# Last pair of up chunks of a streaming-encoder block as a seven-product block pair, with the first tiles of the down product placed on bytes of the pair's operands

## The chip, the cores and the metric

The kernel runs on one core of one Trainium2 chip. The metric is the device time of one execution in microseconds (us). The engines: TensorE (PE) multiplies matrices, VectorE (DVE), ScalarE (ACT) and GpSimd (POOL) do the elementwise work, SyncE (SP) issues most transfers. A time of the trace counts from the first instruction of the profiled execution.

## The reference

The kernel computes one layer of an encoder on 16 meta tokens and 1,024 positions, width 1,024: a mixer (attention with forget gates beside a diagonal state-space model), then a gated feed-forward block with a short causal convolution, then a norm. The change is in the feed-forward block:

```python
def _conv_ffn(xn, w_up, conv_w, conv_b, w_down):
    seq_len = xn.shape[1]
    hid = xn @ w_up
    hp = jnp.pad(hid, ((0, 0), (CONV_WIDTH - 1, 0), (0, 0)))
    conv = conv_b + sum(hp[:, j:j + seq_len] * conv_w[j] for j in range(CONV_WIDTH))
    val, gate = jnp.split(conv, 2, axis=-1)
    return (jax.nn.silu(gate) * val) @ w_down
```

`w_up` is 1024 x 5632, `w_down` 2816 x 1024, all in float32. The layer adds this to its input `h`, the norm is applied to the sum, and the meta tokens are dropped.

## The kernel before

A product of float32 precision is made of three matmuls: each operand is split into a high part (a cast to fp32r on ACT) and a low part (the operand less its high part, a subtraction called a cut here, `split_lo`, L137), and high x high, high x low and low x high are added up in PSUM.

**Up stage.** The 5,632 hidden channels are 22 chunks of values (`ov`) and 22 chunks of gates (`og`), 128 channels each; pair c is value chunk c with gate chunk c. Pairs 0, 1, 2 and 21 are *plain* (`plain_steps`, L1338 to L1366): for each of the two chunks and each of three stretches of 342 positions, 8 slices of the input width times 3 matmuls (L1357 to L1359); the convolution reads PSUM, one activation (L1361) and two products (L1363) for each stretch. Pairs 3 to 20 are *block pairs* (`block_pair`, L1490): the two chunks and the two halves of the positions form a 2 x 2 block product that is made with seven products instead of eight (`seven`, L214; matmuls L236 to L238, additions L242, copies L245 and L250). It reads blocks of the normed input `xhi`/`xlo` (`B11`, `B21`, `B22`; `B12` is not read as such) and four combined blocks `T` (t0 to t3, high and low, 65,792 bytes of each partition, pool `tforms`). The order of the seven is: A11 with B11, S2 with t1, A12 with B21, S3 with t2, S1 with t0, A22 with t3, S4 with B22, two pieces of 258 and 256 columns each. Weight forms are sums on POOL (L1451), casts (L1304) and cuts, in a ring of eight slots (`sw`). Results lie whole in `hg` and `hv`, and one activation and two products for each chunk (L1501, L1503) make the convolution. `glue` (L1311) then applies Silu to the gate, multiplies and stores the chunk to `a_d` in DRAM; for the pairs of `SUMMED` it also stores combined halves to `s_d`.

**Down stage.** The second matmul is again a block product with seven products p, over 11 pairs of rows j = 2c, 2c+1 in four groups: (8, 9), (7, 0, 1), (2, 3, 4), (5, 6, 10). "(g, p)" is product p of group g; the order within a group is 0, 4, 1, 2, 5, 3, 6. `forms(p, j)` loads a weight tile (`wr`, tag "w") and, for a `SUMMED` j, a combined activation tile (`ar`, tags a00 to a11), casts both on ACT (L1583) and cuts them, on POOL for p = 0, 4 and 5, on DVE for the others. The results go into a *slot* of four 128 x 512 tiles; slots are taken from the list `ops` and given back when the product has run. Slots are tiles `op0` to `op5` and quarters of the dead `xhi` and `xlo` (`featq`). `product` runs 4 row tiles x (row pairs of the group) x 3 matmuls of 512 columns (L1697 to L1699) and evicts: (0, 0) by copies on ACT into `u2` (L1702), (0, 1) and (0, 5) by ACT into `hs4` to `hs7` (L1705), all others by additions on DVE (L1707) into `hs`. `hs0` to `hs3` start with the residual, loaded from `h_d` (L1769). Products 4, 5 and 6 add onto PSUM banks of products 0, 1 and 3, so that these must be evicted before.

The order of instructions of an engine is set at build time by a list scheduler from the order of the program, buffers and data; `after(a, b)` adds an order between two instructions. Each engine, and each transfer queue, works in its order. Memory is a stack of pools from the left and from the right; a tile placed on bytes of an earlier one waits for that tile's last use. Before the change `tforms` is closed ahead of the plain pair 21, `down1` (`op0` to `op3`, weights, a tiles) takes its bytes from there on, and `dn` (`gfB`, `sq`, `eps`, `u2`, `hs`, `op4`, `op5`) lies from the end of `down1` over the bytes of the up stage's right side (`st_r`).

## Time and profile before

| | us |
|---|---|
| median of 3 runs | 1427.48 |
| the three runs | 1426.45, 1427.48, 1427.57 |
| the profiled execution, whole time | 1427.24 |
| its span, first to last instruction | 1425.5 |
| granted TensorE clock, mean | 0.998 |

The whole time of the profiled execution contains its span and 1.7 us around it. In a line of a timeline the first number is the start in us, the second the duration, then engine, line, operation, output<-input and shape; what stands in brackets is the idle time of the engine just before and what ended it. A line ending in "q" after the engine's name (SPq) is a transfer's issue. In a group of a line the three numbers behind the count are shortest, median and longest duration in ns.

### The profile page before, as it was taken

The numbers are of one execution on the slowest core, as the hardware profiler recorded it, in microseconds if no ns is written. First come the engines' busy times: TensorE is split into PE (matmuls) and PEld (weight loads), VectorE is DVE, ScalarE is ACT, GpSimd is POOL, SyncE is SP. The second block draws the span as 40 slices with busy tenths as digits, with TensorE's granted clock in tenths as the row PEclk, the third lists the DMA queues.
The fourth block names the chain that finished last, engine by engine and source line by source line (L and its number), as shares of the span: only waits on it lengthen the run. The fifth ranks groups of instructions, "written<-read, shape, count | busy, mean of one in ns | idle before, by whom it ended". The sixth has DMA issues, their size and how long they took to land.

```text
span 1425.5 us, 26319 instructions
## 1 busy us (share of the span) xinstructions
PE 1410.6 (99%) x9607; PEld 1336.1 (94%) x9607; DVE 1070.3 (75%) x2048; ACT 709.0 (50%) x1381; POOL 764.2 (54%) x872
## 2 busy tenths in 40 slices
PE   8999999999999999999999999999999999999997
PEld 8999999988999999999889999999999999888886
DVE  7999889843667675655479977788886776788867
ACT  7647575423555555534546444344444345644444
POOL 1542257642466556326771334545555545888795
PEclk9999999999999999999999999999999999999999
DMA  8685644530156531087953246666753327864443
GB/s 298 176 203 147 160 106 133 172 119 31 53 156 161 127 111 57 23 287 267 216 161 124 73 114 183 183 173 177 178 142 113 98 79 258 327 205 133 129 94 118
DMA packets 93318, 216.17 MB, mean 152 GB/s; under 512 B 14802, under 2 KB 22610, under 8 KB 92804
## 3 DMA queue, kind: packets, MB, share of 16 engines
q1 hardware_dynamic: 74340, 170.28, 36.3%
q0 software_dynamic: 17696, 41.29, 15.1%
q10 hardware_dynamic: 1152, 2.91, 0.7%
q8 instruction: 76, 1.25, 0.4%
q14 instruction: 54, 0.44, 0.1%
HBM read 170.88 MB, written 71.71 MB: 170 GB/s over the span
## 4 chain that ended last, share of the span: by engine, by line
PE 95%; DMA 2%; issue 1%; ACT 1%; DVE 0%; POOL 0%; POOLq 0%; DVEq 0%; SPq 0%
PE mm L174 5%; PE mm L176 5%; PE mm L175 5%; PE sp L236 4%; PE sp L237 4%; PE sp L238 4%; PE tp L236 3%; PE tp L237 3%; PE tp L238 3%; PE mm L238 3%; PE mm L236 3%; PE mm L237 3%; PE po L966 3%; PE tp L920 2%; PE mm L1699 2%; PE mm L1698 2%
## 5 line engine op out<-in xcount | busy, mean ns | idle before, releaser
L174 PE MATMUL mm<-xhi,whi 128*128 128x342 f32 (+2 forms) x480 | 156.1, 325 | 0.0
L175 PE MATMUL mm<-xlo,whi 128*128 128x342 f32 (+2 forms) x480 | 155.4, 324 | 0.0
L176 PE MATMUL mm<-xhi,wlo 128*128 128x342 f32 (+2 forms) x480 | 154.6, 322 | 0.5 <-DMA wlo<-in_w_g_dram 0.5
L1313 POOL TENSOR_TENSOR ov<-ov,og 128x1024 f32<-128x1024 f32 x21 | 50.8, 2421 | 119.7 <-ACT og L1312 117.4
L137 DVE TENSOR_TENSOR sw<-sf,sw 128x512 fp32r<-128x512 f32 x72 | 73.4, 1020 | 46.2 <-ACT sw L1304 45.1
L1304 ACT CAST sw<-sf 128x512 fp32r<-128x512 f32 x72 | 44.9, 624 | 108.9 <-POOL sf L1451 80.1
L176 PEld LDWEIGHTS mm<-xhi,wlo 128*128 128x128 f32 x480 | 90.4, 188 | 1.3 <-DMA wlo<-in_w_g_dram 0.8
L174 PEld LDWEIGHTS mm<-xhi,whi 128*128 128x128 f32 x480 | 90.4, 188 | 1.1 <-issue 0.6
L175 PEld LDWEIGHTS mm<-xlo,whi 128*128 128x128 f32 x480 | 90.4, 188 | 0.4
L1451 POOL TENSOR_TENSOR sf<-raw,sf 128x512 f32<-128x512 f32 x36 | 62.9, 1748 | 38.8 <-DVE sw L137 38.7
L1451 POOL TENSOR_TENSOR sf<-raw 128x512 f32<-128x512 f32 x36 | 49.1, 1363 | 60.0 <-ACT ov L1361 21.5
L238 PE MATMUL mm<-xhi,sw 128*128 128x258 f32 (+1 forms) x288 | 81.0, 281 | 0.0
L236 PE MATMUL mm<-xhi,sw 128*128 128x258 f32 (+1 forms) x288 | 80.8, 280 | 0.0
L237 PE MATMUL mm<-xlo,sw 128*128 128x258 f32 (+1 forms) x288 | 80.7, 280 | 0.0
L883 ACT ACTIVATE pt<-pt,mx 128x400 f32<-128x400 f32 (+5 forms) x72 | 53.1, 737 | 45.2 <-DVE mx L876 44.9
L1503 DVE SCALAR_TENSOR_TENSOR ov<-hv,cwt,ov 128x1024 f32<-128x1024 f32 x36 | 69.9, 1942 | 0.4 <-ACT ov L1501 0.4
L885 POOL TENSOR_SCALAR pt<-pt,mx 128x400 f32<-128x400 f32 (+5 forms) x72 | 51.8, 721 | 33.3 <-DVE mx L884 28.3
L1304 ACT CAST sw<-raw 128x512 fp32r<-128x512 f32 x70 | 43.0, 621 | 45.0 <-PE sp L238 23.1
L137 DVE TENSOR_TENSOR sw<-raw,sw 128x512 fp32r<-128x512 f32 x70 | 57.9, 831 | 4.3 <-ACT sw L1304 4.0
L137 DVE TENSOR_TENSOR tl<-tp,th 128x512 fp32r<-128x512 f32 (+1 forms) x80 | 50.7, 634 | 12.2 <-ACT th L923 11.6
L923 ACT CAST th<-tp 128x512 fp32r<-128x512 f32 (+1 forms) x80 | 43.4, 543 | 32.1 <-PE tp L920 22.7
L852 POOL CAST qz<-q 64x128 fp32r<-64x128 f32 (+1 forms) x72 | 20.2, 283 | 67.2 <-PE sp L871 65.7
(722 smaller groups left out, 5727.2 us busy)
## 6 DMA issues: line engine op xcount, KB each, us to landing
raw<-in_w_up_dram SPq DMA_DIRECT2D x44, 512.0 KB, 3.7
t_d<-in_w_dn_dram POOLq DMA_DIRECT2D x44, 256.0 KB, 6.9
wr<-t_d SPq DMA_DIRECT2D x44, 256.0 KB, 3.4
ar<-a_d SPq DMA_DIRECT2D x41, 256.0 KB, 5.3
a_d<-ov SPq DMA_DIRECT2D x18, 512.0 KB, 2.6
wr<-in_w_dn_dram SPq DMA_DIRECT2D x33, 256.0 KB, 3.8
t_d<-in_w_dn_dram SPq DMA_DIRECT2D x22, 256.0 KB, 4.3
t_d<-t_d SPq DMA_DIRECT2D x22, 256.0 KB, 4.7
```

The costliest lines, as they stand in the source:

```text
L137: return eng.tensor_tensor(out_, src, hi.bitcast(F), ALU.subtract)
L174: yield PE.matmul(ps, whi[:, i, :], ahi[:, i], start=(i == 0), stop=False)
L175: yield PE.matmul(ps, whi[:, i, :], alo[:, i], start=False, stop=False)
L176: yield PE.matmul(ps, wlo[:, i, :], ahi[:, i], start=False, stop=(i == k - 1))
L236: PE.matmul(ps, a[0][:, i], bh, start=(i == 0 and not joins), stop=False, skip_group_check=True)
L237: PE.matmul(ps, a[0][:, i], bl, start=False, stop=False, skip_group_check=True)
L238: PE.matmul(ps, a[1][:, i], bh, start=False, stop=(i == kh - 1), skip_group_check=True)
L883: ends[:] = rd, S.activation(pt[:n, :kc], pt[:n, :kc], AF.Exp, bias=low, scale=-1.0, accum_out=nm[:n, 0:1])
L885: sc_.append(GP.tensor_scalar(pt[:n, :kc], pt[:n, :kc], nm[:n, 1:2], 1.0, ALU.mult, ALU.mult))
L1304: S.copy(hi, src)
L1451: sums.append(GP.tensor_tensor(f_, a, b, op))
L1503: V.scalar_tensor_tensor(out=o, in0=h_[:, j:SEQ + j], scalar=cwc(j, m), in1=o, op0=ALU.mult, op1=ALU.add)
```

## The change

Pair 21 becomes a block pair. `block_pair` is cut in two: the products, and `conv_pair` with the convolution and the glue. `tforms` now stays open through pair 21, and its tiles are placed in the order t1, t2, t0, t3. A small pool `down0` (two weight tiles, two a00 tiles, `eps`) is placed below it, so that it shares no bytes with the up stage. `down1` is placed on the bytes of T in the order weights, a01, `op0`, `op1`, a10, a11, `hs0` to `hs3`, `u2`. The first slots are quarters of `xhi`/`xlo` that the block pairs read no more. At the border the order is: forms (0, 0), products of pair 21, forms (0, 4) and (0, 1), loads of `hs0` to `hs3`, product (0, 0), convolution and glue of pair 21, then the remaining products. Of pair 21's convolution the values come first; the gate's two products on DVE stand behind the cuts so far, the Silu behind the four copies of (0, 0), the first four additions of `hs` behind the gate's last product, the casts of (0, 3) and (0, 6) behind the evictions of (0, 1), the loads of group 0 one behind the other and ahead of the `hs` loads and of group 1, and the cuts of (1, 0) behind those of (0, 5). The last chunk's store goes to POOL's queue instead of ACT's.

```diff
     def glue(g_, v_, c):
-        S.activation(g_, g_, AF.Silu)
+        silu = S.activation(g_, g_, AF.Silu)
+        for cp_ in first_copy:
+            after(silu, cp_)
...
-        (S if c == NFF - 1 else SY).dma_start(rows, v_)
+        (GP if c == NFF - 1 else SY).dma_start(rows, v_)
...
     def conv_out(m, tag):
-        if m % NFF == NFF - 1:
-
-            return ha.tile([P, SEQ], F, tag="h", name=tag, bufs=3, padded_shape=[P, 2 * NH])
...
+    down0 = pool(ctx, "down0", side="left")
+    for tag in ("a00", "w"):
+        down0.tile([P, 512], F, tag=tag, name="hold", bufs=2)
+    eps = down0.tile([P, 1], F, name="eps")
+    V.memset(eps, EPS)
     st_t = ExitStack()
     tq = pool(st_t, "tforms", side="left")
-    T = [[tq.tile([P, KH, NH], R, name=f"t{i}{w}") for w in "hl"] for i in range(4)]
+    T = {i: [tq.tile([P, KH, NH], R, name=f"t{i}{w}") for w in "hl"] for i in (1, 2, 0, 3)}
+    T = [T[i] for i in range(4)]
...
-        res = []
-        for h_, m, tag in ((hg, NFF + c, "og"), (hv, c, "ov")):
-            o = conv_out(m, tag)
+        return hg, hv
+
+    def conv_pair(c, hg, hv, behind=()):
+        res = {}
+        halves = ((hg, NFF + c, "og"), (hv, c, "ov"))
+        for h_, m, tag in halves[::-1] if behind else halves:
+            res[tag] = o = conv_out(m, tag)
             S.activation(o, h_[:, :SEQ], AF.Identity, bias=cwc(3, m), scale=cwc(0, m))
             for j in (1, 2):
-                V.scalar_tensor_tensor(out=o, in0=h_[:, j:SEQ + j], scalar=cwc(j, m), in1=o,
-                                       op0=ALU.mult, op1=ALU.add)
-            res.append(o)
-        glue(*res, c)
+                st_ = V.scalar_tensor_tensor(out=o, in0=h_[:, j:SEQ + j], scalar=cwc(j, m), in1=o,
+                                             op0=ALU.mult, op1=ALU.add)
+                if tag == "og":
+                    for cut in behind:
+                        after(st_, cut)
+                    last_gate[:] = st_,
+        glue(res["og"], res["ov"], c)
...
     for c in range(3, NFF - 1):
-        block_pair(c)
-    st_t.close()
-    plain_pair(NFF - 1)
...
-    down1 = pool(ctx, "down1", side="left")
-    small = [down1.tile([P, 4, 512], R, name=f"op{q}") for q in range(4)]
-    ops = [[t_[:, w] for w in range(4)] for t_ in small]
-    ops += featq
-    dpool = {}
+        conv_pair(c, *block_pair(c))
+
+    def quarter(r, h_):
+        cols = slice((L - 512) * h_, (L - 512) * h_ + 512)
+        return [[t_[:, KH * r + 2 * q + w, cols] for w in range(2) for t_ in (xhi, xlo)] for q in range(2)]
+
+    ops = quarter(0, 1)
...
     def behind(ld, j):
-        if h_load and j in groups[1]:
+        if h_load and len(first_loads) == 12:
             after(ld, h_load[-1])
+        if j in groups[1]:
+            after(ld, first_loads[-1])
+        if j in groups[0]:
+            if first_loads:
+                after(ld, first_loads[-1])
+            first_loads.append(ld)
...
+            if j in groups[0] and p in (3, 6):
+                late_casts.append(hi)
+            elif j in groups[0] and p == 5:
+                fifth[:] = cut,
+            elif j in groups[1] and p == 0:
+                after(cut, fifth[0])
...
+                ev = S.activation(to, ps, AF.Copy, scale=-1.0 if p in MINUS else 1.0)
+                if p == 1:
+                    for hi in late_casts:
+                        after(hi, ev)
             else:
                 first_add.append(V.tensor_tensor(to, to, ps, ALU.subtract if p in MINUS else ALU.add))
+                if len(first_add) <= 4:
+                    after(first_add[-1], last_gate[0])
...
+    ready[0, 0] = [forms(0, j) for j in groups[0]]
+    last_pair = block_pair(NFF - 1)
+    st_t.close()
+    down1 = pool(ctx, "down1", side="left")
     dpool[0] = down1
-    for p in ORDER[:2]:
+    down1.tile([P, 512], F, tag="w", name="hold", bufs=6)
+    down1.tile([P, 512], F, tag="a01", name="hold", bufs=2)
+    small = op_tiles(down1, 0, 2)
+    for tag in ("a10", "a11"):
+        down1.tile([P, 512], F, tag=tag, name="hold", bufs=2)
+    hs = {c: down1.tile([P, D], F, name=f"hs{c}") for c in range(4)}
+    u2 = [down1.tile([P, 512], F, name=f"u2{c}") for c in range(4)]
+    ops += small + quarter(0, 0) + quarter(1, 0)
+    for p in (4, 1):
         ready[0, p] = [forms(p, j) for j in groups[0]]
+    for c in range(4):
+        h_load.append(SY.dma_start(hs[c], h_d[P * c:P * c + P]))
+        after(h_load[-1], first_loads[-1])
+    product(0, 0, ready[0, 0], True, False)
+    conv_pair(NFF - 1, *last_pair, behind=cuts)
     st_r.close()
     dn = pool(ctx, "down", side="left")
...
+    ops += op_tiles(dn, 2, 4) + quarter(1, 1) + op_tiles(dn, 4, 6)
+    hs.update((c, dn.tile([P, D], F, name=f"hs{c}")) for c in (4, 5))
+    cuts.clear()
+    ops += ready[0, 0]
+    for g, p in turns[1:]:
         prepare()
```

More of the change, by code (lines that the diff above doesn't have):

```diff
@@ L1512, in block_kernel, with weight_tile, raw_buffer, op_tiles @@
     for c in range(3, NFF - 1):
-        block_pair(c)
-    st_t.close()
-    plain_pair(NFF - 1)
-    down1 = pool(ctx, "down1", side="left")
-    small = [down1.tile([P, 4, 512], R, name=f"op{q}") for q in range(4)]
-    ops = [[t_[:, w] for w in range(4)] for t_ in small]
-    ops += featq
-    dpool = {}
+        conv_pair(c, *block_pair(c))
[3 more added lines that the diff above has]
+    ops = quarter(0, 1)
+    n_w = [0]
+    def weight_tile():
+        n_w[0] += 1
+        if n_w[0] % 8 in (1, 2):
+            return down0.tile([P, 512], F, tag="w", name="wr", bufs=2)
+        return down1.tile([P, 512], F, tag="w", name="wr", bufs=6)
+    def raw_buffer(j, tag):
+        pl = dpool[turn_of[j] % 4 // 2]
+        if pl is dpool[0] and tag == "a00":
+            pl = down0
+        return pl.tile([P, 512], F, tag=tag, name="ar", bufs=2)
+    def op_tiles(pl, q0, q1):
+        small = [pl.tile([P, 4, 512], R, name=f"op{q}") for q in range(q0, q1)]
+        return [[t_[:, w] for w in range(4)] for t_ in small]
+    dpool = {0: None}
     pairs = {}
@@ L1593, in forms @@
         return slot
[L1595 removed]
+    first_add, cuts, late_casts, fifth = [], [], [], []
     held = {}
@@ L1758, in block_kernel @@
     gfB = dn.tile([P, D], F, name="gfB")
-    dn.tile([P, 512], F, tag="a00", name="hold", bufs=2)
+    for tag in ("a00", "a01", "a10", "a11"):
+        dn.tile([P, 512], F, tag=tag, name="hold", bufs=2)
+    hs.update((c, dn.tile([P, D], F, name=f"hs{c}")) for c in (7, 6))
     sq = dn.tile([P, 512], BF, name="sq")
-    eps = dn.tile([P, 1], F, name="eps")
-    V.memset(eps, EPS)
-    u2 = [dn.tile([P, 512], F, name=f"u2{c}") for c in range(4)]
-    hs = [dn.tile([P, D], F, name=f"hs{c}") for c in range(4)]
-    hs += [dn.tile([P, D], F, name=f"hs{c}") for c in range(4, KD)]
-    small2 = [dn.tile([P, 4, 512], R, name=f"op{q}") for q in range(4, 6)]
-    ops += [[t_[:, w] for w in range(4)] for t_ in small2]
-    for c in range(4):
-        h_load.append(SY.dma_start(hs[c], h_d[P * c:P * c + P]))
-    for g, p in turns:
+    ops += op_tiles(dn, 2, 4) + quarter(1, 1) + op_tiles(dn, 4, 6)
[3 more added lines that the diff above has]
+    for g, p in turns[1:]:
         prepare()
```

13 lines of the change are left out of this document (6 added, 7 removed).

## The prediction

> **What bounds the kernel now.** I read the page first, then the waits of PE, then PE's timeline around the last pair of up chunks.
>
> ```profile
> span 1425.5 us, 26319 instructions
> PE 1410.6 (99%) x9607; PEld 1336.1 (94%) x9607; DVE 1070.3 (75%) x2048; ACT 709.0 (50%) x1381; POOL 764.2 (54%) x872
> PE 95%; DMA 2%; issue 1%; ACT 1%; DVE 0%; POOL 0%; POOLq 0%; DVEq 0%; SPq 0%
> PE mm L355 <- ACT uh L413: 5.2, 1, 5.2
> PE mm L1208 <- DVE olo L137: 0.6, 1, 0.6
> PE mm L176 <- DMA wlo<-in_w_g_dram: 0.5, 1, 0.5
> PE sp L870 <- DVE mx L876: 0.3, 1, 0.3
> PE tp L236 <- DVE ms L242: 0.2, 1, 0.2
> ```
>
> PE is busy 99% of the span, 95% of the chain that ended last is PE, and the five rows of waits are all that PE waits for in the whole run: 6.8 us, of which 5.2 come at the start. Busy PE time is modelled, so the test is the spacing of starts. PE's timeline has these at the edges:
>
> ```profile
> 1143.99 0.28 PE L236 MATMUL mm<-xhi,sw 128*128 128x258 f32 x1
> 1163.95 0.28 PE L236 MATMUL mm<-xhi,sw 128*128 128x258 f32 x1
> 1183.93 0.32 PE L1357 MATMUL mm<-xhi,sw 128*128 128x344 f32 x1
> 1206.63 0.40 PE L1697 MATMUL mm<-op 128*128 128x512 f32 x1
> 1417.07 0.28 PE L1699 MATMUL mm<-xlo 128*128 128x224 f32 x1
> ```
>
> Block pair 19 starts at 1143.99, pair 20 at 1163.95, the plain pair 21 at 1183.93, the down stage at 1206.63, and its last matmul at 1417.07, 8.4 us before the span ends. Between these marks I compared each start with the next: of the 1,086 matmuls from 1183.93 to 1417.07 none starts more than 0.03 us later after the one before it than is usual for its width. So PE has nothing to win at the border but work, and all that feeds it is hidden there. The same stretches by engine (columns: length, then busy us of PE, PEld, DVE, ACT, POOL, then clock, DMA share, GB/s):
>
> ```profile
> 1143.99:1163.95 19.96, 19.96 (x170) 19.96 (x169) 16.63 (x23) 8.87 (x14) 8.72 (x6) 1.00 0.24 80
> 1163.95:1183.93 19.98, 19.98 (x170) 19.98 (x169) 11.87 (x19) 7.59 (x13) 6.81 (x5) 1.00 0.29 102
> 1183.93:1206.63 22.70, 22.70 (x146) 22.70 (x145) 13.91 (x19) 13.60 (x22) 15.69 (x9) 1.00 0.79 282
> 1206.63:1212.07 5.44, 5.44 (x26) 4.51 (x25) 4.87 (x8) 3.33 (x7) 0.00 (x0) 1.00 0.77 243
> 1216.16:1245.50 29.34, 29.34 (x130) 24.21 (x129) 24.27 (x28) 18.52 (x35) 25.99 (x18) 1.00 1.00 367
> ```
>
> **What the change takes off PE.** The plain pair is 2 chunks x 3 stretches x 8 x 3 = 144 matmuls of some 342 columns: 22.70 us, 158 ns each. A block pair is 7 products x 2 pieces x 4 x 3 = 168 matmuls of 258 or 256 columns: 19.96 and 19.98 us in the two rows, 119 ns each. (The counts of the rows hold one or two that overlap the edge.) The 24 extra matmuls and their weight loads are in these rows. PE's work falls by 22.70 - 19.97 = **2.73 us**. Products of the down stage stay as many and as wide: 24 matmuls of 512 columns for two row pairs are 5.44 us. Nothing else of the change removes PE work, so 2.73 us is the ceiling, and everything below asks how much of it a new wait takes back.
>
> At this place a rule of the Trainium skill speaks against the change. TensorE: Matmul & The Clock Gate, section "Back-to-back issue gap", gives for a stream of weight load and matmul pairs a sustained spacing of about 81 ns at 128 columns and 131 ns at 512; on a straight line between them I estimate 109 ns at 343 and 98 ns at 257, so the last pair would go from 15.7 to 16.4 us, 0.7 us slower. The trace doesn't agree: 158 and 119 ns, and 5.44/24 = 227 ns at 512.
>
> **What must now be ready, and when.** In the new order the last pair starts at 1183.93 and ends at 1203.9; product (0,0) runs to 1209.3, (0,4) to 1214.8, (0,1) to 1220.2, (0,2) to 1225.7, (0,5) to 1231.1, (0,3) to 1236.6, (0,6) to 1242.0. Before, the T forms were dead during the plain pair, and the down stage's first tiles lay there from 1183 on. Now T is read to near the pair's end. When, the last reads in pair 20 say:
>
> ```profile
> L236 PE MATMUL sp<-t1h,sw x144: 278/281/286, 827.1 to 1169.3; 128*128 128x258 f32 x72, 128*128 128x256 f32 x72
> L236 PE MATMUL sp<-t2h,sw x144: 277/282/367, 832.8 to 1175.4; 128*128 128x258 f32 x72, 128*128 128x256 f32 x72
> L236 PE MATMUL tp<-t0h,sw x144: 277/282/286, 835.7 to 1177.9; 128*128 128x258 f32 x72, 128*128 128x256 f32 x72
> L236 PE MATMUL sp<-t3h,sw x144: 276/282/293, 838.5 to 1180.7; 128*128 128x258 f32 x72, 128*128 128x256 f32 x72
> ```
>
> Shifted by 19.98: t1 is free at 1189.3, t2 at 1195.4, t0 at 1197.9, t3 at 1200.7. The new order of T in memory (1, 2, 0, 3) and of `down1` puts weights and `a01` on t1, `op0`/`op1` on t2, `a10`/`a11` and `hs0`/`hs1` on t0, `hs2`/`hs3` and `u2` on t3. The prices of the steps, from the timelines of ACT, DVE and SP, the list of DMA issues from 1150 on, and the view of L137:
>
> ```profile
> 1186.04 1.24 ACT L1501 ACTIVATE og<-hg,cwt 128x1024 f32<-128x1024 f32 x1
> 1191.11 1.06 ACT L1312 ACTIVATE og<-og 128x1024 f32<-128x1024 f32 x1 [0.50 <-DVE og L1503]
> 1199.89 0.61 ACT L1583 CAST xhi<-ar 128x512 fp32r<-128x512 f32 x1
> 1212.90 1.08 ACT L1702 COPY u<-mm 128x512 f32<-128x512 f32 x2 [2.94 <-DVE eps L1762]
> 1183.08 1.28 DVE L1503 SCALAR_TENSOR_TENSOR ov<-hv,cwt,ov 128x1024 f32<-128x1024 f32 x1
> 1211.28 1.23 DVE L1313 TENSOR_TENSOR ov<-ov,og 128x1024 f32<-128x1024 f32 x1
> 1207.52 8.95 SPq L1769 DMA_DIRECT2D hs<-h_d  x4
> wr<-t_d SPq DMA_DIRECT2D x14, 256.0 KB, 5.9
> hs<-h_d SPq DMA_DIRECT2D x4, 512.0 KB, 5.2
> L137 DVE TENSOR_TENSOR xhi<-ar,xhi x6: 683/692/1403, 1203.6 to 1236.2; 128x512 fp32r<-128x512 f32 x6
> L137 DVE TENSOR_TENSOR xlo<-wr,xlo x4: 678/938/1784, 1221.7 to 1249.0; 128x512 fp32r<-128x512 f32 x4
> L137 POOL TENSOR_TENSOR op<-ar,op x8: 1289/1302/2292, 1185.5 to 1240.4; 128x512 fp32r<-128x512 f32 x8
> ```
>
> The last three rows are the cuts (the line that makes the low part of an operand) between 1183.9 and 1250, with shortest/median/longest in ns: on DVE 0.68 us at the quick price and 1.78 at the slow one, on POOL 1.29 and 2.29.
>
> Step by step, against the starts above:
> - **Weight forms of pair 21**: 7 casts, 7 cuts and 4 POOL sums instead of 4 and 4, during pair 20. The stretch of pair 19 carries such a set with DVE 16.63 and POOL 8.72 of 19.96 us; pair 20's has room. Nothing.
> - **(0,0)** takes its slots in `xhi`/`xlo`, rows 0 to 3, columns from 528, which no block pair reads, and its tiles in `down0`. Its 4 loads, 4 casts and 4 POOL cuts (9.2 us at 2.29) lie under pairs 20 and 21: needed at 1203.9. Nothing.
> - **(0,4)**: weights and `a01` load from 1189.3, landing by 1195.2 (5.9 us); `op0` is free at 1195.4; 4 casts 2.4 us, 4 POOL cuts 5.2 to 9.2 us: ready by 1207, needed at 1209.3. POOL is otherwise free.
> - **(0,1)**: `a10` loads from 1197.9, lands by 1203.8; casts to 1206.3; DVE cuts 4 x 0.68 = 2.7 or 4 x 1.78 = 7.1 us: 1209 to 1213.6, needed at 1214.8.
> - **hs loads** wait for t3, 1200.7, and stand on SP ahead of the loads of (0,2) and (0,5). At the 367 GB/s of the last window, 2.1 MB are 5.7 us and each product's 1.05 MB 2.9 us: hs by 1206.4, before the first add at 1210.7; (0,2) by 1209.3, its casts by 1211.7, its cuts by 1214.4 to 1218.8, needed at 1220.2; (0,5) by 1212.2, its casts by 1214.6, its POOL cuts by 1219.8 to 1223.8, needed at 1225.7.
> - **The last pair's convolution**: two activations of 1.24 and four products of 1.28 on whole rows take the place of 6 and 12 small ones. The gate's two wait on DVE behind the four cuts of (0,1), and behind them wait the first four adds: gate by 1212 to 1216. The adds free the banks of (0,2), needed at 1220.2: 4 x 0.69 fit. Silu waits on ACT for the four copies of (0,0), 1210; behind it casts of (0,2). The product (1.23) and the store follow by 1218; the store stands on POOL's queue, ahead of cuts of (0,5) at worst, which then still end by 1223 to 1227. The chunk is read only in the last group.
> - **(0,3)**: its casts wait for ACT's evictions of (0,1), 1220.8; casts to 1223.3, DVE cuts to 1226 or 1230.4, needed at 1231.1. (0,6) follows by 1229 to 1237.5, needed at 1236.6.
> - **Group 1's** loads now stand behind all of group 0's and partly lie on `og`, `ov`, `hg`, `hv` bytes, free by 1218; its first cuts on POOL stand behind those of (0,5). Needed at 1242: 6 cuts are 7.7 to 13.7 us. Hidden.
> - **eps** is set early. ACT's 2.94 us wait behind it goes, but no PE wait hung on it: nothing.
>
> Every cover holds at the quick price of a cut, and by about 1 us even where all four cuts are slow; only the store, (0,6) and two slow stretches in a row pass their time, by 1 to 2 us. The unknown is thus bounded by 0 below (no PE gap to remove) and, above, by the second rival's 7.6 us. I take 0: the medians of the three rows of cuts, 0.69, 0.94 and 1.30, lie by the quick price. Sum: 1427.24 us, the profiled execution's own time (span 1425.5 and 1.7 around it), less 2.73 = 1424.5; on the median of the three runs, 1427.48, that is **1424.7**.
>
> **Rivals.**
> - *A short wait*: one of the late cuts (slow price, 1.78 or 2.29) leaves PE waiting up to 2.7 us. For it: the cushion shrinks, since operands no longer have a plain pair's 22.70 us in dead T bytes. Against: the medians of the cuts. 1425.3 to 1427.5.
> - *Slower: SP's queue jams at the hs loads.* Before, the four took 8.95 us to issue, as their buffers weren't free. If t3 or the order holds SP as long again, (0,2) and (0,5), queued behind, are 9 us later than above. (0,2) has a margin of 1.4 us with slow cuts and 5.8 with quick ones, so PE waits 3.2 to 7.6 us. From 2.73 on the change loses: +0.5 to +4.9, 1428.0 to 1432.4. Against: the last read of t3 is PE's own, 3 us before the pair ends, so that nothing slow holds those bytes.
> - *The count of matmuls sets the time, not their columns*: at the plain pair's 158 ns, 168 are 26.5 us, 3.8 us more than before: 1431.3. Against: pairs 19 and 20 run at 119 ns; 108 ns between 257 and 512 columns is 0.42 ns a column, which leaves 10 ns of fixed part. The Trainium skill's rule above leans to this side.
> - *Another end*: the order of the last group shifts with the new slots, and the 8.4 us behind the last matmul change by some tenths, either way: 1423.8 to 1425.
>
> **How the numbers follow.** About 0.2%, 2.85 us, is what a measurement of this kernel can tell from no change; the ceiling of 2.73 lies just inside it, so the forecast itself is "within", with a good part of its scatter beyond. Forecast: 0.60 (0.22 of it beyond the bound, 0.38 within). Short wait: 0.16, within. Jam: 0.17 (0.11 slower, with waits over 5.6 us, which the slow cuts of a crowded stretch would give; 0.06 within). Count: 0.01, slower. Another end: 0.06 (0.04 faster, 0.02 within). Faster 0.26, same 0.62, slower 0.12. The forecast's own range is 1424.2 to 1425.3; to 8 in 10 it takes in the short wait and the lower end of the jam: 1424.0 to 1428.6.
>
> **What would show it.** Right: the first 512-column matmul comes 19.9 to 20.0 us after the start of pair 21, and PE's waits show no new row from there on. Wrong: rows of PE waiting for DVE or POOL in L137, for ACT in L1583, or for DVE in L1707 between 1204 and 1250; then the gap before (0,4), (0,1), (0,5) or (0,3) names the step. A jam would show as a long SP issue of `hs<-h_d`. A last pair of 22 us or more would bear out the count.

## The result: slower, and the profile after

| | before | after |
|---|---|---|
| median of 6 runs, us | 1426.28 | 1436.59 |
| lowest and highest | 1425.76 to 1427.57 | 1435.86 to 1437.07 |
| the profiled execution, whole time | 1427.24 | 1437.07 |
| its span | 1425.5 | 1435.3 |

The ratio after to before is 1.007 (95% interval 1.0057 to 1.0083). The kernel became 10 us slower where 2.7 us less was forecast. (Of the ten executions of the later run before_quarter one was slow, 2820.56 us; its ratio below is that of the other nine.) The waits of PE in the kernel after (first number: us in total, then how often, then the longest):

```profile
PE mm L355 <- ACT uh L413: 5.1, 1, 5.1
PE mm L1740 <- DVE hs L1753: 3.9, 1, 3.9
PE mm L236 <- ACT c L245: 2.8, 3, 1.4
PE mm L1741 <- DVE xlo L137: 0.5, 1, 0.5
...
```

Three rows are new. The two of L1740 and L1741 (the down stage's matmuls, L1697 and L1698 before) are where the prediction had said to look; the row of L236 is in the block pairs, where it had said nothing. Where in time the loss lies, the table by stretches tells. Both kernels are cut at the first matmul of pair 3, the first of the down stage, and the last of all. Columns: length, then busy us and instructions of PE, PEld, DVE, ACT, POOL, then clock, DMA share, GB/s. Before, then after:

```profile
824.28:1206.63 382.35, 382.35 (x3170) 382.33 (x3169) 294.43 (x396) 167.68 (x272) 200.95 (x148) 1.00 0.54 153
1206.63:1417.07 210.44, 210.44 (x944) 174.31 (x942) 166.76 (x210) 96.46 (x189) 166.28 (x120) 1.00 0.53 168
```

```profile
822.78:1206.57 383.79, 380.94 (x3194) 380.14 (x3193) 295.76 (x395) 161.64 (x266) 196.05 (x149) 1.00 0.51 143
1206.57:1427.35 220.78, 216.42 (x944) 176.16 (x942) 177.00 (x215) 103.67 (x199) 175.99 (x125) 0.98 0.55 175
1186.60:1206.57 19.97, 19.97 (x170) 19.97 (x169) 11.27 (x19) 7.26 (x12) 2.74 (x2) 1.00 0.39 132
```

The last row is pair 21: 19.97 us, as forecast. So the saving of 2.73 us is there, and the up part should have taken 382.35 - 2.73 = 379.62 us. It took 383.79: **4.2 us are lost in the up part** (loss A). The down stage has the same 944 matmul records as before and takes **10.3 us more**. Of these, 4.4 are idle time of PE (220.78 less 216.42 busy); the other 6 are in matmuls that start further apart. Summed from PE's timeline by the starts, some 5.0 of the 10.3 us are gaps, 2.8 are a lower clock behind the longest gap (together loss B, 7.8), and 2.5 are spread over all matmuls of the stage (loss C). Less 2.73, plus 4.2, plus 10.3 is +11.8; the block pairs had begun 1.5 us earlier in this execution, which leaves the 10.28 us between the two last matmuls.

**Loss A in the timeline.** PE and ACT around the largest of the three waits, in pair 19 of the kernel after:

```profile
1148.93 0.28 PE L238 MATMUL sp<-t1h,sw 128*128 128x256 f32 x1
1150.58 0.39 PE L236 MATMUL mm<-xhi,sw 128*128 128x258 f32 x1 [1.37 <-ACT c L245]
```

```profile
1145.01 0.60 ACT L1304 CAST sw<-raw 128x512 fp32r<-128x512 f32 x1
1149.03 1.24 ACT L1511 ACTIVATE og<-hg,cwt 128x1024 f32<-128x1024 f32 x1 [3.41 <-issue]
1150.17 0.63 ACT L245 COPY c<-mm 128x258 f32<-128x258 f32 x2
```

```profile
1148.45 0.41 DVE L242 TENSOR_TENSOR hg<-tp,hg 128x256 f32<-128x256 f32 x1
```

and ACT at the same place of the kernel before:

```profile
1145.68 0.38 ACT L245 COPY c<-mm 128x258 f32<-128x258 f32 x1 [0.81 <-PE mm L238]
1146.43 1.25 ACT L1501 ACTIVATE og<-hg,cwt 128x1024 f32<-128x1024 f32 x1 [0.38 <-DVE hg L242]
1147.58 0.35 ACT L245 COPY c<-mm 128x256 f32<-128x256 f32 x1
```

The copies empty PSUM banks that PE needs. Before, one stands ahead of the activation `og<-hg` and one behind it; after, both stand behind it. ACT is idle for 3.4 us, PE waits, and the activation starts at 1149.03, just behind DVE's last addition to `hg`, which ends at 1148.86. (The profile names no releaser for this idle time, "issue"; that it was `hg` is read from these two times.) The other two waits are at 1128 and 1170, in pairs 18 and 20. Nothing in pairs 18 to 20 was edited, but the list scheduler had the forms of (0, 0) to place among them and ordered the rest anew.

**Loss B in the timeline.** DVE in the kernel after, from the last cut of (0, 2) on:

```profile
1223.24 1.78 DVE L137 TENSOR_TENSOR xlo<-ar,xhi 128x512 fp32r<-128x512 f32 x1
1228.22 1.88 DVE L1753 TENSOR_TENSOR u<-u,mm 128x512 f32<-128x512 f32 x3 [3.20 <-PE mm L1742]
1230.02 0.68 DVE L1753 TENSOR_TENSOR u<-u,po 128x512 f32<-128x512 f32 x1
1230.62 0.68 DVE L137 TENSOR_TENSOR xlo<-ar,xhi 128x512 fp32r<-128x512 f32 x1
1231.22 1.79 DVE L137 TENSOR_TENSOR xlo<-wr,xhi 128x512 fp32r<-128x512 f32 x1
...
1243.14 1.75 DVE L137 TENSOR_TENSOR xlo<-ar,xhi 128x512 fp32r<-128x512 f32 x1
1244.81 1.27 DVE L1753 TENSOR_TENSOR hs<-hs,mm 128x512 f32<-128x512 f32 x2
```

and PE:

```profile
1241.26 0.40 PE L1741 MATMUL tp<-xlo,xhi 128*128 128x512 f32 x1
1245.54 0.79 PE L1740 MATMUL mm<-op 128*128 128x512 f32 x1 [3.89 <-DVE hs L1753]
...
1246.56 0.63 PE L1742 MATMUL mm<-op 128*128 128x512 f32 x1
1246.98 0.63 PE L1740 MATMUL mm<-op 128*128 128x512 f32 x1
```

DVE is idle for 3.2 us with the additions of (0, 2), which wait for PE, at the head of its queue. Then come nine cuts, eight of them at the slow price, from 1230.62 to 1244.81, and only then the additions that empty the banks of (0, 3), onto which (0, 6) adds. PE waits for the first of these: 4.28 us lie between its starts at 1241.26 and 1245.54, a gap of 4.05 beyond the usual 0.23. Then 14 matmuls start some 0.43 us apart. In windows of 10 us (columns as above):

```profile
1226.00:1236.00 10.00, 10.00 (x44) 7.83 (x42) 7.78 (x8) 7.64 (x15) 8.04 (x7) 1.00 0.97 337
1236.00:1246.00 10.00, 5.64 (x23) 4.32 (x23) 10.00 (x8) 6.09 (x12) 10.00 (x7) 0.94 0.86 300
1246.00:1256.00 10.00, 10.00 (x33) 7.89 (x33) 10.00 (x12) 4.38 (x8) 8.17 (x7) 0.72 0.72 221
```

In the second window DVE and POOL are both busy throughout, and together they do 8 + 7 = 15 instructions.

### The profile page after: what moved, and what is told of

It reads as the page before. It is cut to its first block, busy times and chain, and to the rows that moved or that the text cites. A ratio compares the mean times of both kernels' runs of the same rounds, so it can differ in the third digit from the quotient of the medians.

```text
span 1435.3 us, 26376 instructions
## 1 busy us (share of the span) xinstructions
PE 1414.5 (99%) x9631; PEld 1335.2 (93%) x9631; DVE 1080.5 (75%) x2053; ACT 709.9 (49%) x1384; POOL 768.7 (54%) x877
## 4 chain that ended last, share of the span: by engine, by line
PE 94%; DVE 2%; DMA 1%; issue 1%; ACT 1%; POOL 0%; POOLq 0%; DVEq 0%; SPq 0%; ACTq 0%
PE mm L174 5%; PE mm L175 5%; PE mm L176 5%; PE sp L236 4%; PE sp L237 4%; PE sp L238 4%; PE tp L236 3%; PE tp L237 3%; PE tp L238 3%; PE mm L236 3%; PE mm L238 3%; PE mm L237 3%; PE po L966 3%; PE tp L920 2%; PE mm L1740 2%; PE mm L1741 2%
## 5 line engine op out<-in xcount | busy, mean ns | idle before, releaser
L137 DVE TENSOR_TENSOR sw<-sf,sw 128x512 fp32r<-128x512 f32 x76 | 79.8, 1050 | 56.2 <-ACT sw L1304 56.1
L236 PE MATMUL mm<-xhi,sw 128*128 128x256 f32 (+1 forms) x304 | 85.7, 282 | 2.8 <-ACT c L245 2.8
L238 PE MATMUL mm<-xhi,sw 128*128 128x256 f32 (+1 forms) x304 | 85.5, 281 | 0.0
L237 PE MATMUL mm<-xlo,sw 128*128 128x256 f32 (+1 forms) x304 | 85.3, 280 | 0.0
L1513 DVE SCALAR_TENSOR_TENSOR ov<-hv,cwt,ov 128x1024 f32<-128x1024 f32 x38 | 74.2, 1954 | 0.0
L236 PEld LDWEIGHTS mm<-xhi,sw 128*128 128x128 f32 x304 | 57.2, 188 | 3.4 <-ACT c L245 3.4
```

The source lines that it names most:

```text
L137: return eng.tensor_tensor(out_, src, hi.bitcast(F), ALU.subtract)
L236: PE.matmul(ps, a[0][:, i], bh, start=(i == 0 and not joins), stop=False, skip_group_check=True)
L237: PE.matmul(ps, a[0][:, i], bl, start=False, stop=False, skip_group_check=True)
L238: PE.matmul(ps, a[1][:, i], bh, start=False, stop=(i == kh - 1), skip_group_check=True)
L1513: st_ = V.scalar_tensor_tensor(out=o, in0=h_[:, j:SEQ + j], scalar=cwc(j, m), in1=o, op0=ALU.mult, op1=ALU.add)
```

## The experiments

The theories. For A: the new order of the up stage, brought about by the early forms of (0, 0); rival: the block pair itself. For B: (B1) a wait of casts behind evictions; (B2) the price of cuts while DVE and POOL cut at the same time; (B3) the order in DVE's and ACT's queues; (B4) the sum of the work, which has lost its head start. For C: (C1) 32 bytes of alignment; (C2) slots that lie half in `xhi`, half in `xlo`; (C3) where the tiles of a slot begin. (The expectations of thin_pool, dve1, hold_part_dve1 and hold_dve2 call the price of cuts B3, and B4 operands that are late by loads and casts; that of align calls C1 C.) All runs were timed beside the kernel before on the same chip:

| label | us, median (range) | ratio to before, 95% |
|---|---|---|
| hold00 | 1432.64 (1432.04 to 1434.19) | 1.0049 (1.0034 to 1.0064) |
| align | 1435.39 (1434.38 to 1437.43) | 1.0068 (1.0051 to 1.0085) |
| block_only | 1434.39 (1432.48 to 1436.02) | 1.0059 (1.0044 to 1.0074) |
| free_late | 1436.64 (1435.69 to 1438.75) | 1.0077 (1.0062 to 1.0092) |
| part | 1436.92 (1436.74 to 1439.46) | 1.0082 (1.0067 to 1.0097) |
| thin_pool | 1429.76 (1428.62 to 1430.43) | 1.0026 (1.0016 to 1.0036) |
| dve1 | 1436.0 (1434.64 to 1437.22) | 1.0068 (1.0051 to 1.0085) |
| hold_part_dve1 | 1433.53 (1432.67 to 1434.21) | 1.0053 (1.0038 to 1.0068) |
| before_quarter | 1429.79 (1428.8 to 2820.56) | 1.0026 (1.0016 to 1.0036) |
| hold_dve2 | 1432.21 (1431.65 to 1433.35) | 1.0044 (1.003 to 1.0058) |
| hold_thin | 1426.05 (1424.45 to 1428.15) | 0.9998 (0.9988 to 1.0007) |
| hold_silu | 1437.24 (1435.36 to 1438.0) | 1.0074 (1.0059 to 1.0089) |
| hold_silu_dve2 | 1432.17 (1431.31 to 1433.07) | 1.0041 (1.0027 to 1.0055) |
| before_pitch | 1431.27 (1429.69 to 1434.45) | 1.0039 (1.0026 to 1.0052) |
| before_128 | 1432.6 (1430.24 to 1432.98) | 1.0047 (1.0031 to 1.0064) |
| before_inter | 1426.49 (1425.32 to 1427.6) | 1.0001 (0.9992 to 1.0011) |
| hold_dve2_fifth | 1428.63 (1427.13 to 1429.62) | 1.0015 (1.0005 to 1.0024) |
| hold_dve2_fifth_late | 1429.73 (1429.6 to 1431.01) | 1.0027 (1.0016 to 1.0039) |

### Loss A: hold00

From the kernel after; the forms of (0, 0) are emitted behind the products of pair 21, and their casts follow its last weight cast.

```diff
-        S.copy(hi, src)
+        w_casts.append(S.copy(hi, src))
...
+            if j in groups[0] and p == 0:
+                after(hi, w_casts[-1])
...
-    ready[0, 0] = [forms(0, j) for j in groups[0]]
     last_pair = block_pair(NFF - 1)
+    ready[0, 0] = [forms(0, j) for j in groups[0]]
```

> The loads, casts and cuts of (0,0) are emitted behind the products of pair 21, and each of its casts is ordered behind pair 21's last weight cast; all else as in the changed kernel. Theory A (the four casts and cuts of (0,0), put among the weight forms of pairs 18 to 20, make the three waits of PE for the copy c at L245, 3.9 us with what follows each): pairs 3 to 20 take 359.6 us again and the time falls by 3.5 to 4.2 us, to 1432.4 to 1433.1, if the rest stays. Rival (the new memory below T, or the new border as a whole, disturbs the pairs): the three waits stay and the time is 1436 to 1437.

The time falls by 3.95 us against the kernel after, to 1432.64. The same cut into stretches:

```profile
822.87:1202.81 379.94, 379.94 (x3194) 379.89 (x3193) 298.22 (x395) 162.59 (x266) 201.34 (x149) 1.00 0.51 142
1202.81:1422.69 219.88, 214.94 (x943) 175.13 (x942) 179.10 (x215) 104.26 (x199) 177.70 (x125) 0.99 0.57 180
```

The up part is 379.94 us, 20.0 for each of 19 block pairs, and no wait at L236 is left. Loss A is shown: it is the early forms of (0, 0), not the block pair. The down stage keeps its 219.88.

### Does the border's new order bring the loss: block_only

The kernel before with nothing but the block pair for pair 21:

```diff
+    block_pair(NFF - 1)
     st_t.close()
-    plain_pair(NFF - 1)
```

> The kernel before with pair 21 as a block pair and nothing else of the change: T is freed by pair 21, and the down stage's first tiles lie on it as before. What the new order was for: operands of (0,0) wait for t0 (14 us into pair 21) and its a tiles for t2 (11 us), so its casts come at the pair's end and its POOL cuts 5 to 9 us later; PE waits 8 to 12 us at the border and runs at a lower clock behind it: 1432 to 1439. Rival (the border is as well covered as the prediction took it to be, and only the new order does harm): 1423.5 to 1425.

1434.39 us, with an up part of 380.16 us and a down stage of 221.20. PE's waits are many and short; the first two:

```profile
PE mm L1696 <- POOL op L137: 2.0, 2, 1.0
PE sp L1696 <- DVE xhi L137: 1.7, 1, 1.7
...
```

So taking the plain pair away costs 10.8 us at the border by itself (221.20 against 210.44), and its matmuls far from the border are no further apart than before (441 from 1285 to 1385): operands of the first products were prepared beside the plain pair's 22.70 us, in bytes that T now holds. The order of the change gathers these waits into one and makes the loss there smaller (7.8), but it adds A and C.

### Where the wait comes from: free_late

```diff
-            if j in groups[0] and p in (3, 6):
-                late_casts.append(hi)
-            elif j in groups[0] and p == 5:
+            if j in groups[0] and p == 5:
```

> The casts of (0,3) and (0,6) are no longer ordered behind ACT's evictions of (0,1). Theory B1 (DVE stood idle from 1225.0 to 1228.2 because its cuts of (0,3) came late and behind the additions of (0,2), and so the nine cuts ahead of the addition that PE waited for ended late): the cuts start 3 us or more sooner, the 4 us wait of PE and the 3 us of lower clock behind it shrink by half or more, 1430 to 1433. Rival B2 (the nine cuts at 1.78 us, beside POOL's, are the cause by themselves): the wait stays and the time is 1435 to 1438.

The wait ahead of (0, 6) is gone and the time is the same, 1436.64 us:

```profile
PE sp L1740 <- DVE xlo L137: 2.3, 1, 2.3
PE sp L1738 <- DVE hs L1751: 1.1, 1, 1.1
```

These now stand near 1270 to 1281. B1 falls as the cause of the loss, which only moved on, by some 30 us.

### The price of a cut: thin_pool, hold_thin

```diff
-            cut = split_lo(eng, slot[q + 1], src, slot[q])
+            thin = slice(0, 32 if j in groups[1] and p in (0, 4) else 512)
+            cut = split_lo(eng, slot[q + 1][:, thin], src[:, thin], slot[q][:, thin])
```

> POOL's cuts of (1,0) and (1,4) cover 32 of 512 columns, so the low parts of these operands are left out; POOL's load between 1229 and 1250 falls by some 18 us. Theory B3 (DVE's cuts cost 1.78 us instead of 0.68 because POOL cuts at the same time; eight of them stand ahead of PE's (0,6)): they cost 0.7 us, PE's waits of 4.7 us around (0,6) and the lower clock behind them go, 1427 to 1430. Rival B4 (operands are late by the loads and the casts, whatever a cut costs): the cuts stay where they are and PE waits as long: 1434 to 1437.

The edit leaves out 480 of 512 columns of twelve cuts on POOL; DVE's own cuts are all there. 1429.76 us, 6.8 less than the kernel after, and no wait of PE in the down stage. The cuts of one form on DVE from 1226 to 1256 (shortest, median, longest in ns), in the kernel after and then in thin_pool:

```profile
L137 DVE TENSOR_TENSOR op<-wr,op x4: 678/1764/1779, 1238.1 to 1255.3; 128x512 fp32r<-128x512 f32 x4
```

```profile
L137 DVE TENSOR_TENSOR op<-wr,op x4: 678/709/740, 1235.0 to 1251.2; 128x512 fp32r<-128x512 f32 x4
```

The same instruction on tiles of the same names goes from 1.76 to 0.71 us when POOL has little to cut beside it. In the kernel after, every cut on DVE from 1206 to 1256 that took over 1 us overlaps with work of POOL. That is B2, and it is as large as nearly all of loss B. hold_thin has the edits of hold00 as well:

> The held forms of (0, 0) together with the thinned POOL cuts of (1, 0) and (1, 4): 32 of 512 columns, the low parts of those operands are left out. If the up stage's loss and the border's are independent and the slots' cut is the third, the two gains add: 1432.64 - (1436.59 - 1429.76) = 1425.8, no wait of PE behind pair 18, and matmuls of the down stage still 0.231 us apart. If the border's wait only comes up elsewhere once the up stage is faster: 1429 and more.

```profile
822.63:1202.42 379.79, 379.79 (x3194) 379.79 (x3193) 297.43 (x395) 162.61 (x266) 200.14 (x149) 1.00 0.51 142
1202.42:1415.47 213.05, 213.05 (x943) 174.25 (x942) 166.73 (x215) 103.92 (x199) 162.59 (x125) 1.00 0.57 186
```

1426.05 us against 1425.8 expected: A and B add, PE is busy in every microsecond of both stretches, and what is left is +2.6 in the down stage (loss C) against -2.6 in the up part. Together they make no difference to the kernel before.

### POOL's cuts on DVE: dve1, hold_part_dve1, hold_dve2

```diff
-        eng = GP if p in (0, 4, 5) else V
+        eng = GP if p in (0, 4, 5) and not (j in groups[1] and p in (0, 4)) else V
```

> The twelve cuts of (1,0) and (1,4) are made on DVE instead of POOL, all computed in full. Under B3 one cut on each engine at the same time takes 1.78 us and one after the other on DVE 0.6 each, so DVE gets through its 8 cuts of group 0 and these 12 in 12 to 13 us instead of 14 us for the 8: PE's wait before (0,6) shrinks to under 1 us, and the time falls by 4 to 8 us, to 1428 to 1432. Under B4, or if DVE is short of time itself, 12 more cuts of 0.6 us on the busier engine make it slower: 1437 to 1443.

1436.0 us; the wait ahead of (0, 6) is gone, and one as large stands near 1258 instead:

```profile
PE tp L1740 <- DVE u L1753: 4.7, 1, 4.7
```

The same with the edits of hold00 and part (below):

> The three edits together: (0,0)'s casts and cuts behind pair 21's weight forms, slots wholly in xhi or xlo, cuts of (1,0) and (1,4) on DVE. If A, B3 and C2 hold and add up, 3.5 + 4 to 8 + 2 to 2.7 us go: 1422.5 to 1427, at or below the kernel before (1425.65 in the last series). If the loss at the border only moves on, as with the casts set free, 1429 to 1433.

1433.53 us, with the same wait of 4.7 us. Then all cuts of group 1 and of (0, 5) on DVE, with hold00:

```diff
-        eng = GP if p in (0, 4, 5) else V
+        eng = GP if p in (0, 4, 5) and not (j in groups[1] or j in groups[0] and p == 5) else V
```

> (0,0)'s casts and cuts behind pair 21's weight forms, and all cuts of group 1 and those of (0,5) on DVE, so that POOL has only sums between 1215 and 1300. Under B3 a cut on POOL holds both engines for 1.25 to 1.75 us and one on DVE for 0.6, so 22 moved cuts give back some 14 us of the two engines' common time, nearly what the run with POOL's cuts left out gave: no PE wait over 1 us in the down stage and 1425.5 to 1428. If DVE's own time is short (rival), the wait moves on once more: 1431 to 1434.

1432.21 us. The waits, and the window with the lower clock:

```profile
PE sp L1745 <- DVE op L137: 2.9, 1, 2.9
PE tp L1744 <- DVE u L1757: 1.0, 1, 1.0
```

```profile
1226.00:1236.00 10.00, 7.42 (x25) 5.95 (x26) 10.00 (x18) 6.94 (x13) 0.00 (x0) 0.83 0.87 293
```

DVE alone does 18 instructions in this window, with POOL idle; in the kernel after, the two together did 15 in the same time. (The window after is that from 1236.) So giving POOL a share of the cuts made the whole slower here. Yet the time hardly moved, and DVE's own timeline says why:

```profile
1219.34 0.69 DVE L137 TENSOR_TENSOR xlo<-ar,xhi 128x512 fp32r<-128x512 f32 x1
1224.84 1.88 DVE L1757 TENSOR_TENSOR u<-u,mm 128x512 f32<-128x512 f32 x3 [4.81 <-PE mm L1746]
...
1227.24 0.69 DVE L137 TENSOR_TENSOR op<-ar,op 128x512 fp32r<-128x512 f32 x1
```

DVE is idle for 4.8 us with the additions of (0, 2) at the head of its queue, and the cuts of (0, 5), for which PE then waits, stand behind them. This looks like B3.

### The order of the queues: hold_silu, hold_silu_dve2, hold_dve2_fifth, hold_dve2_fifth_late

First ACT's queue: it stood 4.3 us ahead of pair 21's Silu, with casts behind it. The edit, on hold00 and on hold_dve2:

```diff
+            if j in groups[0] and p == 2:
+                after(silus[-1], hi)
```

> The held forms of (0, 0), and pair 21's Silu ordered behind the casts of (0, 2) on ACT instead of ahead of them. In the run of the held forms with group 1's cuts on DVE, ACT stood still for 4.3 us ahead of that Silu, with the casts of (0, 2) and (0, 5) queued behind it. Theory that this queue is what delays the operands: casts and cuts come some 4 us earlier, the 4.05 us wait ahead of (0, 6) and the slow matmuls behind it go: 1426 to 1428. Theory that DVE and POOL together cannot cut fast enough, whenever the casts come: the wait stays or moves, 1431 to 1434.

> As the run before it, with all cuts of group 1 and of (0, 5) on DVE. Theory of the queue: without the Silu ahead of the casts DVE has no 4.8 us of idle time at 1220, the two waits of PE (3.0 and 1.1 us) go, 1427 to 1429. Theory that the sum of the DVE work is the limit (it was busy from 1225 to 1276 without a break): the waits shrink by less than half, 1430 to 1432.

1437.24 and 1432.17 us: the first is 4.6 slower than hold00, the second the same as hold_dve2. ACT in hold_silu:

```profile
1214.40 1.06 ACT L1316 ACTIVATE og<-og 128x1024 f32<-128x1024 f32 x1
1222.67 0.62 ACT L1625 CAST xhi<-wr 128x512 fp32r<-128x512 f32 x1 [7.22 <-DMA wr<-in_w_dn_dram]
```

The Silu comes earlier, but the list now has a cast at the head of ACT's queue whose weights land only at 1222.6, and ACT stands 7.2 us there. PE then waits 3.4 us for evictions on ACT behind it. Moving the Silu is no remedy, but since the new stall came with it, these two runs don't show what the Silu's place costs by itself. Then DVE's queue: the additions of (0, 2) ordered behind the cuts of (0, 5), on hold_dve2.

```diff
                 if len(first_add) <= 4:
                     after(first_add[-1], last_gate[0])
+                elif len(first_add) <= 8:
+                    after(first_add[-1], fifth[0])
```

> As the held forms with group 1's and (0, 5)'s cuts on DVE, but the four additions of (0, 2) are ordered behind the cuts of (0, 5) on DVE. There DVE stood still for 4.8 us at 1220 with those additions at its head, while the casts for the cuts of (0, 5) were done by 1219. Theory that the order of DVE's queue makes the wait: PE's waits of 2.9 and 1.0 us and the lower clock behind the first (1.5 us) go, 1427 to 1428.5. Theory that the sum of the DVE work is the limit: the wait returns at a later product, 1430 to 1432.

1428.63 us, 3.6 less than hold_dve2 and 8.0 less than the kernel after, with nothing left out. One wait of PE remains from 1100 on, and the clock stays full:

```profile
PE tp L1744 <- DVE u L1757: 1.6, 1, 1.6
```

```profile
824.95:1204.74 379.79, 379.79 (x3194) 379.79 (x3193) 294.79 (x395) 162.82 (x265) 200.34 (x149) 1.00 0.51 142
1204.74:1419.84 215.10, 213.53 (x943) 174.12 (x942) 180.50 (x237) 103.10 (x199) 145.89 (x103) 1.00 0.57 184
```

The down stage is 4.7 over that of before: 1.6 of waiting, the rest nearly all loss C. B is therefore a matter of two things together, the price of cuts that run on both engines, and the order of DVE's queue. POOL's cuts on DVE alone moved the wait (dve1, hold_dve2); with the new order as well, most of it went. The new order with the cuts left on POOL was not run, so the share of each stays open. The last run also takes the edit of free_late:

> The same with the casts of (0, 3) and (0, 6) no longer ordered behind the evictions of (0, 1), so that the cuts of (0, 3) also stand in DVE's idle time at 1220. Theory of the order: no wait of PE behind pair 21 at all, 1426.5 to 1428, with the spacing of 0.231 us the only thing left. Theory of the sum: 1429 to 1432.

1429.73 us, with a wait of 2.4 us for DVE's additions near 1242: a miss, since the cuts of (0, 3) that came forward push others back. Some of the lost head start (B4) stays as a wait of 1.6 to 2.4 us. No order tried here beats the kernel before.

### Loss C: align, part, before_quarter, before_pitch, before_128, before_inter

The matmuls of 512 columns start 0.2275 us apart before and 0.231 after, from 1285 to 1385, far from every wait. First the kernel after with `eps` of 64 bytes, so that every tile above lies 32 bytes on, and with slots wholly in `xhi` or wholly in `xlo`:

```diff
-    eps = down0.tile([P, 1], F, name="eps")
+    eps = down0.tile([P, 16], F, name="eps")[:, :1]
```

```diff
-        return [[t_[:, KH * r + 2 * q + w, cols] for w in range(2) for t_ in (xhi, xlo)] for q in range(2)]
+        return [[t_[:, KH * r + w, cols] for w in range(KH)] for t_ in (xhi, xlo)]
```

> The eps tile takes 64 bytes of a partition instead of 32, so that all tiles above it move by 32 bytes; every engine's order is that of the changed kernel. Theory C (matmuls of the down stage start 0.230 us apart instead of 0.2275 because their operands lie 32 bytes off a multiple of 64): the spacing of matmuls on op tiles goes back to 0.2275, and the time falls by 1.5 to 2.5 us to about 1434.5. Rival (the spacing comes from the split of a slot over xhi and xlo, or from traffic): no change, 1436 to 1437.

> The first slots are the same bytes of xhi and xlo, but one slot lies wholly in xhi and the other wholly in xlo, as the slots of the kernel before did; before, each slot took its high tiles from xhi and its low tiles from xlo. Theory C2 (it is this mixture that makes matmuls of the down stage start 0.231 us apart instead of 0.2275): the spacing between 1285 and 1385 goes back to 0.2275 to 0.228, worth 2 to 2.7 us: 1433.5 to 1434.5 where the changed kernel gives 1436 to 1436.6. Rival (the spacing hangs on where the op tiles lie, or on traffic): 0.230 to 0.231 again, no change in time.

Both stayed at 0.231 us (1435.39 and 1436.92): C1 and C2 fall. Then the kernel before with its eight slots in `xhi` and `xlo` cut in other ways, instead of four tiles of 512 columns side by side (`ops += featq`):

```diff
-    ops += featq
+    ops += quarter(0, 1) + quarter(0, 0) + quarter(1, 0) + quarter(1, 1)
```

```diff
-    ops += featq
+    ops += [[flat(t_)[:, 2080 * q + 520 * w:2080 * q + 520 * w + 512] for w in range(4)]
+            for t_ in (xhi, xlo) for q in range(4)]
```

```diff
-    ops += featq
+    ops += [[flat(t_)[:, c0:c0 + 512] for w in range(4) for c0 in [2048 * q + 512 * w + 32 * (q + w // 2)]]
+            for t_ in (xhi, xlo) for q in range(4)]
```

```diff
-    ops += featq
+    ops += [[flat(t_)[:, 2048 * w + 512 * q:2048 * w + 512 * q + 512] for w in range(4)]
+            for t_ in (xhi, xlo) for q in range(4)]
```

> The kernel before, with the eight slots in xhi and xlo cut as the changed kernel cuts them (rows of 4,160 bytes, columns 0 to 511 and 528 to 1039) instead of as runs of 2,048 bytes. Theory C3 (this cut of the slots, not their mixture, makes the down stage's matmuls start 0.231 us apart instead of 0.2275): spacing 0.230 to 0.231 between 1285 and 1385, 2 to 3 us slower than before, 1427.7 to 1428.7. Rival (the place of the op tiles or of other tiles in memory does it): 0.2275 and 1425.5 to 1426.2.

> The kernel before with its eight slots in the dead xhi and xlo as four tiles side by side as they were, but 2,080 bytes apart instead of 2,048. If the spacing of the matmuls depends on where the tiles of a slot begin in steps of 2,048 bytes, it widens from 0.2275 toward 0.231 us as with the quarters: 1428 to 1430. If what widens it is that a quarter's tiles lie in two tensors, far apart, nothing changes: 1425.5 to 1427.

> The kernel before with its eight slots in the dead xhi and xlo as four tiles side by side, but the third and the fourth tile (the second operand) moved by 128 bytes against the first two, and each slot by 128 more. Theory of the 2,048 byte grid: the spacing between two matmuls on these slots widens from 0.2270 toward 0.231 us, as with 2,080 bytes. Theory that a multiple of 128 bytes is enough (2,080 is none, and a quarter's rows of 4,160 bytes are none): it stays at 0.2270, and the time at 1425.5 to 1427.

> The kernel before with the four tiles of each of the eight slots 8,192 bytes apart in the same tensor instead of side by side: every tile stays on the 2,048 byte grid. Theory of the grid, or of 128 bytes: spacing 0.2270 us, 1425.5 to 1427. Theory that tiles must lie side by side: it widens toward 0.231, 1428 to 1430.

The 100 us from 1285 to 1385, PE busy throughout and at full clock; the first bracket counts the matmuls. Before, then after:

```profile
1285.00:1385.00 100.00, 100.00 (x442) 82.47 (x440) 79.14 (x91) 41.86 (x80) 80.55 (x60) 1.00 0.45 124
```

```profile
1285.00:1385.00 100.00, 100.00 (x435) 81.33 (x434) 74.65 (x87) 39.57 (x74) 79.69 (x61) 1.00 0.48 131
```

before_quarter, before_128 and before_inter:

```profile
1285.00:1385.00 100.00, 100.00 (x435) 81.38 (x434) 77.63 (x91) 41.05 (x77) 79.49 (x59) 1.00 0.44 124
```

```profile
1285.00:1385.00 100.00, 100.00 (x437) 81.67 (x436) 77.18 (x91) 40.68 (x76) 81.06 (x59) 1.00 0.46 126
```

```profile
1285.00:1385.00 100.00, 100.00 (x441) 82.51 (x440) 78.61 (x91) 41.78 (x80) 81.63 (x60) 1.00 0.46 124
```

before_pitch has 436. With quarters, with tiles 2,080 bytes apart and with tiles shifted by 128 bytes the stage does 435 to 437 matmuls in 100 us; with tiles that keep steps of 2,048 bytes from each other, side by side or 8,192 apart, 441 or 442. So for the slots in `xhi` and `xlo` it is where the tiles of a slot begin, in steps of 2,048 bytes from each other (C3), not that they lie together, nor a multiple of 128 bytes. 1.6% of some 210 us is 3.3 us, close to the 2.6 of hold_thin. The three off the grid were 3.9, 5.0 and 6.4 us slower than the kernel before, more than that: their lists of instructions differ a little too, and PE waits 0.7, 1.5 and 2.8 us in them. What in the chip makes it so, the runs don't say.

C3 isn't all of loss C. Split by tile in PE's timeline from 1270 to 1400, the step from one matmul on tiles in `xhi` or `xlo` to the next such matmul is 226.9 ns in the kernel before, 232.2 in before_quarter and 229.7 in the kernel after. From one matmul on `op` tiles to the next it is 228.6, 229.4 and 230.8. An `op` slot is four tiles side by side in all three kernels, so the cut of the slots doesn't explain these 2.2 ns. With 185 of 563 steps there, they are an estimated quarter of loss C, and that part stays open.

## Why the prediction was wrong, point by point

- **What the change takes off PE**: right. Pair 21 took 19.97 us, and with A held off 19 pairs took 379.8 to 379.9.
- **Pair 20 has room, "Nothing", and (0, 0), "Nothing"**: wrong, 4.2 us. The engines had room, as the stretches said. But the order is made by a list, and work put into pairs 18 to 20 changed where ACT's copies stand against an activation that waits. Busy shares can't show this. hold00 removed it.
- **(0, 4), (0, 1), (0, 2), (0, 5)**: right in effect. PE waits for none of them. (Pair 21 began at 1186.60, so times of the run lie 2.7 us behind those of the prediction here and below.) The Silu was put behind the copies, at 1210; in the run it waited 4.27 us behind them for the gate's products, to 1217.5.
- **hs loads and the jam rival**: the loads were issued in 2.77 us, not 8.95, so the rival's mechanism did not happen:

```profile
1202.38 2.77 SPq L1816 DMA_DIRECT2D hs<-h_d  x4
```

- **(0, 3), and (0, 6), which "follows by 1229 to 1237.5, needed at 1236.6"**: this is the step that failed most, and the sum carried it as the term put at 0. Its slow end took four slow cuts for each product one after the other, from 1223 on. In the run DVE first stood behind the additions of (0, 2), began only at 1230.6, and had nine cuts, not eight, eight of them slow; and the additions of (0, 3), which the step did not name as queued behind these cuts, came at 1244.8. The choice "I take 0", because the medians of the cuts lay by the quick price, read a price as a property of the instruction. It was one of what POOL does at the time. POOL's cuts of group 1, "Hidden" in the prediction, ran beside them: of DVE's cuts from 1206 to 1256, 5 of 26 took over 1.6 us before and 13 of 23 after, though POOL made much the same number (18 and 20).
- **The unknown bounded above "by the second rival's 7.6 us"**: the waits with the clock behind them cost 7.8. The size was met by chance, the mechanism was another, and A and C came on top. The short wait rival ("one of the late cuts") had the right instruction, but one wait of at most 2.7 us.
- **"Products of the down stage stay as many and as wide"**: true, but 2.5 us are lost all the same, in good part since the new slots are off the 2,048 byte steps. No step looked at where the slots lie.
- **The count of matmuls**: it did not set the time; 168 took 19.97 us.

## What to carry to other kernels

Work taken off a saturated engine also takes away cover: price what was prepared beside it, queue by queue and with the price an operation has while its neighbour engine runs the same kind, not with its median. After an edit, compare each engine's order also where nothing was edited, since a list scheduler may have moved a copy behind a wait. When tiles of matmul operands move, measure the spacing of matmuls far from any wait.

## What the runs showed of the hardware

- **Cuts on DVE and POOL at the same time**: 18 cuts and additions in 10 us on DVE alone, 15 on both together. The Trainium skill, GPSIMD Engine Reference, section "Specifications", says that GpSimd's memory interfaces are shared with VectorE and that they contend with VectorE instructions of two inputs from SBUF; a cut is one, and the trace agrees (0.71 against 1.76 us on DVE).
- **The clock behind a wait**: after the 4.05 us gap 14 matmuls stood some 0.43 us apart, about half speed; in hold00, behind a gap as long, it was 6. The Trainium skill, TensorE: Matmul & The Clock Gate, section "What's actually happening", has the clock halve after an idle window of about 3.4 us. The size agrees; the length doesn't agree as a threshold: in hold_dve2 a gap of 3.02 us was enough (clock 0.83 in its window) and in free_late one of 2.47, while in before_128 one of 2.94 was followed by full speed.
- **The steps between operands**: 442 against 435 matmuls in 100 us (before and before_quarter), for tiles on and off steps of 2,048 bytes. No run tells the cause.
